# Attention probabilities turned by DMA transposes in place of TensorE transposes

## The chip, the cores and the metric

The kernel runs on one core of a Trainium2 chip. The metric is device time in microseconds (us) of one execution. The engines are TensorE (PE; its weight loads are listed apart as PEld), VectorE (DVE), ScalarE (ACT), GpSimd (POOL) and SyncE (SP). SP, ACT and POOL also issue DMA transfers, each in the order of its own queue; an entry that waits for something holds back all entries behind it on that queue.

## The reference

One decoder layer on 1024 tokens of width 1024. A normalised input is projected once; the columns feed two mixers, whose outputs are gated, projected, merged and added to the input. The part that matters here is mixer A: three groups of sliding-window attention with different window and dilation, eight heads each.

```python
qkv = dsa_qkv.astype(f32).reshape(b, s, DSA_GROUPS, 3, DSA_HEADS, DSA_HEAD_DIM)
q_a = _apply_rope(qkv[:, :, :, 0], cos, sin)
k_a = _apply_rope(qkv[:, :, :, 1], cos, sin)
v_a = qkv[:, :, :, 2]
# per group (window, dilation) = (128,1), (512,4), (2048,16):
scores = jnp.einsum('brnqhd,brnkhd->brnhqk', qb, kb) * (dh ** -0.5)
scores = jnp.where(valid[:, None], scores, -jnp.inf)
m = jnp.max(scores, axis=-1, keepdims=True)
p = jnp.exp(scores - m)
den = jnp.sum(p, axis=-1, keepdims=True)
o = jnp.einsum('brnhqk,brnkhd->brnqhd', p / den, vb)
# the three groups are merged by weights proportional to their denominators
```

Mixer B (gated DeltaNet), the gates and the output projection come after the attention stretch or share TensorE with it.

## The kernel before, in words

All projections run as split products: each float32 operand is written as a high and a low float16 part (`hi`, `lo`), and one product is three float16 matmuls (hi times hi, hi times lo, lo times hi; lines 182 to 184). The columns are cut in units of 256. For mixer A there is one q, one k and one v unit for each of six sets `(g, hs)`: group g in the order 2, 1, 0, and half hs of the heads (four heads each). A class `Feed` holds the units in order; one `tick` of it emits three matmuls of 512 columns or their equal. Weights of a unit come through two buffers `wstage` (one DMA each, issued by POOL, lines 161 and 312), and ACT and DVE split them into `whi` and `wlo`.

A finished q or k unit is rotated by DVE and ACT (`rope_half`) into tiles `pch`/`pcl`, and `rope_out` carries it in pieces of 32 partitions to the tiles `Qh`, `Ql` and `Ks`: 16 DMAs for a unit, and 2 more that copy a half for a q unit (lines 624 and 627).

Attention of one set is the generator `att_run`. It takes 16 steps: eight blocks j of 128 queries, and for each two passes `par`, with two heads in each (u = 0, 1). `nk` is the number of 128-key blocks that a query block sees: one in group 2, one or two in turn in group 1, two in group 0 except for the first block. A step s has three parts:

- `scores(s)`: four matmuls into a PSUM bank `ps_S` (two banks); then for each head a DVE instruction that masks, negates and takes the extreme in one go and writes the tile `sm` (line 794, called the reduce below), and an ACT exponential in place with its sum (line 798).
- `turn(s)`: PE transposes the probabilities, one 128x128 float32 block at a time, into a PSUM bank `ps_G` (line 808); ACT copies them to float16 (`th`, line 813), and DVE writes the remainder (`tl`).
- `values(s)`: matmuls of `th` and `tl` with the values `Vh`, `Vl` into the one bank `ps_O` (lines 831 to 835).

Iteration s of the loop emits `scores(s)`, `turn(s-1)` and `values(s-2)`, and yields a number of ticks (`pace`) behind each; `feed.run` puts that many ticks of projection matmuls there. PE's order is thus written out by hand. The order on DVE, ACT, POOL and SP is set by a scheduler that honours priorities; buffers (`bufs=2` and the like) add waits between engines. Results of groups 2 and 1 go to DRAM (`og`), and `combine` loads them back while group 0 runs (line 865, on SP).

Of the kernel before, what the change touches and what calls it, by code (L numbers as in the profile page):

```python
# [10 lines left out]
F32 = mybir.dt.float32  # L11
# [66 lines left out]
def hybrid_block(ctx: ExitStack, tc: tile.TileContext, A):  # L78
# [540 lines left out]
    def rope_out(pt, pieces):  # L619

        with tc.high_priority():
            for name, dst, r0, _ in pieces:
                for hd in range(4):
                    nc.sync.dma_start(out=dst[r0:r0 + 32, hd], in_=pt[name[1]][32 * hd:32 * hd + 32, "AB".index(name[0])])  # L624
# [128 lines left out]
    def att_run(g, hs, ts, pace):  # L753
# [17 lines left out]
        def scores(s):  # L771
# [10 lines left out]
            for u in range(2):  # L782
# [5 lines left out]
                          skip_group_check=True)  # L788
            P = ap.tile([128, 2, 256], F32, name="sm", tag="sm", bufs=2)
            Ps[s] = P  # L790
            for u in range(2):
                hd = 2 * u + par
                with tc.high_priority():
                    V.tensor_tensor_reduce(P[:, u, :128 * nk], psc[:, u * 256:u * 256 + 128 * nk], mask,  # L794
                                           -cexp, -NEG, ALU.add, ALU.min, accum_out=osb[:, 256 + hd:257 + hd])
            for u in range(2):
                hd = 2 * u + par
                SC.activation(P[:, u, :128 * nk], P[:, u, :128 * nk], AF.Exp, bias=osb[:, 256 + hd:257 + hd],  # L798
                              scale=-1.0, accum_out=osb[:, 260 + hd:261 + hd])

        def turn(s):
            nk = len(blocks(steps[s][0]))
            P = Ps.pop(s)
            pt = bank("G", 2)
            for u in range(2):
                for i in range(nk):
                    c = (u * nk + i) * 128
                    PE.transpose(pt[:, c:c + 128], P[:, u, i * 128:i * 128 + 128], ident)  # L808
            n = 256 * nk
            th = ap.tile([128, 512], F16, name="th", tag="th", bufs=2)  # L810
            tl = ap.tile([128, 512], F16, name="tl", tag="tl", bufs=2)
            with tc.high_priority():
                SC.copy(th[:, :n], pt[:, :n])  # L813
                TT(tl[:, :n], pt[:, :n], th[:, :n], ALU.subtract)
            ths[s] = th, tl

        def values(s):
            j, par = steps[s]
            kb = blocks(j)
            nk = len(kb)  # L820
            th, tl = ths.pop(s)
            if par == 0:
                pos[j] = bank("O", 1)
            po = pos[j]
            for u in range(2):
                hd = 2 * u + par
                out = po[:, hd * 64:hd * 64 + 64]
                vs = slice(hd * 64, hd * 64 + 64)
                for i, b in enumerate(kb):
                    c = slice((u * nk + i) * 128, (u * nk + i) * 128 + 128)  # L830
                    PE.matmul(out, lhsT=th[:, c], rhs=Vh[:, b, vs], start=(hd == 0 and i == 0), stop=False,
                              skip_group_check=True)
                    PE.matmul(out, lhsT=th[:, c], rhs=Vl[:, b, vs], start=False, stop=False,
                              skip_group_check=True)
                    PE.matmul(out, lhsT=tl[:, c], rhs=Vh[:, b, vs], start=False, stop=(i == nk - 1),
                              skip_group_check=True)
# [71 lines left out]
    gsp = {}  # L908
    gpool = [rp, "gst", 1]

# [21 lines left out]
    def gate_spill(br, dt, hf, p, rest=None):  # L932
        if (br, dt) not in gsp:
            gsp[br, dt] = tc.dram_tile([128, S], F32, name=f"gsp{br}{dt}")
        t = gpool[0].tile([128, 512], F32, name="gst", tag=gpool[1], bufs=gpool[2])
        if rest is not None:
# [114 lines left out]
    pre.append(pp_)  # L1051
    gpool[:] = pp_, "gst", 1
    def by_chunk(dst, x, hbs=(0, 1)):
# [585 lines left out]
    late.append(fp)  # L1639
    gpool[:] = fp, "gst", 2  # L1640
    gctx.close()
# [344 lines left out]
```

## Time and profile before

| | us |
|---|---|
| median of 3 runs | 1082.25 |
| the three runs | 1080.16, 1082.25, 1085.16 |
| span of the profiled execution | 1083.1 |
| PE busy in it | 1052.6 |
| DVE busy in it | 854.9 |
| ACT busy in it | 559.6 |
| POOL busy in it | 66.5 |

No time outside the span is listed for the profiled execution; its span stands 0.85 us above the median of the runs. Attention runs from about 100 us to 552 us of the span. In the views, a group row reads: line, engine, operation, tiles written and read, shape, count | busy us in all, mean ns of one | idle time of the engine ahead of them and what ended it. A window row reads: stretch, length, busy us (and count) of PE, PEld, DVE, ACT, POOL, then granted clock, DMA share and GB/s. Matmuls overlap in the pipeline, so the distance from one start to the next tells what one costs PE.

### The profile page before, as it was taken

The page shows a single profiled execution, that of the slowest core. Times are in us where ns is not written, and L with a number is a line of the kernel's source. Part 1 is how long each engine was busy: PE and PEld are TensorE (multiplying, and loading weights), DVE is VectorE, ACT ScalarE, POOL GpSimd, SP SyncE. Part 2 cuts the span into 40 slices and gives each one's busy share as a digit, 9 for nine tenths or more (in the row PEclk, how much of TensorE's full clock was granted, in tenths as well). Part 3 has the DMA queues.
Part 4 walks back from the last instruction along what each step waited for, and adds up shares of the span by engine and source line. Part 5 has one row for each costly group of instructions (what it writes and reads, how often), then busy time and mean ns, then how long its engine had stood idle before and what let it go on. Part 6 is the DMA issues. An engine that isn't in the chain of part 4 may idle for free.

```text
span 1083.1 us, 23724 instructions
## 1 busy us (share of the span) xinstructions
PE 1052.6 (97%) x9426; PEld 641.4 (59%) x9426; DVE 854.9 (79%) x1967; ACT 559.6 (52%) x1272; POOL 66.5 (6%) x115
## 2 busy tenths in 40 slices
PE   6999999999999999999999999999999999999997
PEld 6894595775966855765645544555545554444443
DVE  5697897878879778979965797976588778799934
ACT  6445766667666565557645534244454345333622
POOL 1200000000000000000000000110200000000000
PEclk9999999999999999999999999999999999999999
DMA  8135531632724431741233457785685523753232
GB/s 295 60 98 136 128 109 55 167 99 66 190 79 132 101 126 47 182 117 59 75 122 136 111 130 175 250 247 159 195 269 167 147 99 101 285 185 123 83 120 78
DMA packets 99632, 148.99 MB, mean 138 GB/s; under 512 B 31152, under 2 KB 64432, under 8 KB 98368
## 3 DMA queue, kind: packets, MB, share of 16 engines
q1 hardware_dynamic: 69264, 85.20, 27.3%
q0 software_dynamic: 12320, 44.11, 13.5%
q10 hardware_dynamic: 17936, 18.16, 4.9%
q8 instruction: 74, 1.21, 0.5%
q14 instruction: 38, 0.31, 0.1%
HBM read 91.66 MB, written 36.90 MB: 119 GB/s over the span
## 4 chain that ended last, share of the span: by engine, by line
PE 59%; DVE 26%; DMA 5%; ACT 4%; issue 3%; SPq 2%; ACTq 0%; DVEq 0%
PE ps_mm L182 14%; PE ps_mm L184 14%; PE ps_mm L183 14%; DVE ca L83 4%; DVE wlo L83 2%; DVE X L86 2%; DVE stmp L86 2%; DVE sm L794 2%; DVE rt L86 2%; PE ps_S L182 1%; PE ps_S L184 1%; PE ps_S L183 1%; DVE tl L86 1%; PE ps_G L808 1%; SPq L624 1%
## 5 line engine op out<-in xcount | busy, mean ns | idle before, releaser
L184 PE MATMUL ps_mm<-h_hi,wlo 128*128 128x512 f16 (+1 forms) x552 | 208.6, 378 | 1.2 <-issue 1.2
L183 PE MATMUL ps_mm<-h_lo,whi 128*128 128x512 f16 (+1 forms) x492 | 185.9, 378 | 1.0 <-DVE h_lo L86 1.0
L182 PE MATMUL ps_mm<-h_hi,whi 128*128 128x512 f16 (+1 forms) x492 | 186.0, 378 | 0.9 <-ACT h_hi L434 0.9
L184 PEld LDWEIGHTS <-wlo 128*128 128x128 f16 x788 | 77.5, 98 | 89.5 <-issue 3.4
L182 PEld LDWEIGHTS <-whi 128*128 128x128 f16 x848 | 83.4, 98 | 70.8 <-issue 0.5
L183 PEld LDWEIGHTS <-whi 128*128 128x128 f16 x848 | 83.4, 98 | 69.1 <-issue 2.2
L182 PE MATMUL ps_mm<-whi,h_hi 128*128 128x256 f16 x384 | 105.1, 274 | 0.0
L798 ACT ACTIVATE sm<-sm,osb 128x128 f32<-128x128 f32 (+1 forms) x160 | 69.5, 435 | 68.7 <-DVE osb L794 62.0
L184 PE MATMUL ps_mm<-whi,h_lo 128*128 128x256 f16 x384 | 104.7, 273 | 0.0
L183 PE MATMUL ps_mm<-wlo,h_hi 128*128 128x256 f16 x384 | 104.7, 273 | 0.0
L86 DVE TENSOR_TENSOR tl<-ps_G,th 128x256 f16<-128x256 f32 (+1 forms) x96 | 51.8, 540 | 21.5 <-ACT th L813 21.0
L794 DVE CUSTOM_DVE_ANT_0 sm<-ps_S,amask 128x128 f32<-128x128 f32 (+1 forms) x192 | 59.2, 345 | 8.5 <-PE ps_S L787 8.3
L83 DVE SCALAR_TENSOR_TENSOR wlo<-wstage,whi 128x1024 f16<-128x1024 f32 x50 | 60.8, 1218 | 4.4 <-ACT whi L165 4.1
L83 DVE SCALAR_TENSOR_TENSOR ca<-xc,cw,ca 128x512 f32<-128x512 f32 x72 | 53.7, 746 | 7.1 <-ACT ca L1001 6.3
L165 ACT ACTIVATE whi<-wstage 128x1024 f16<-128x1024 f32 x49 | 51.3, 1051 | 3.0 <-PE ps_O L183 1.4
L83 DVE SCALAR_TENSOR_TENSOR whi<-wstage,whi 128x512 f16<-128x512 f32 x60 | 40.8, 687 | 13.6 <-ACT whi L329 12.9
L808 PE MATMUL ps_G<-cons,sm 128*128 128x128 f32 x280 | 47.5, 275 | 2.1 <-ACT sm L798 1.0
L183 PEld LDWEIGHTS <-h_hi 128*128 128x128 f16 x384 | 45.8, 119 | 1.6
L329 ACT ACTIVATE whi<-wstage 128x512 f16<-128x512 f32 x60 | 37.1, 626 | 18.5 <-DVE wstage L328 13.4
L182 PE MATMUL ps_mm<-h_hi,wlo 128*128 128x512 f16 x120 | 45.6, 380 | 1.0 <-DVE rx L83 1.0
L182 PEld LDWEIGHTS <-h_hi 128*128 128x128 f16 x384 | 45.5, 119 | 1.5
L184 PEld LDWEIGHTS <-h_lo 128*128 128x128 f16 x384 | 45.5, 119 | 1.5
(436 smaller groups left out, 2584.4 us busy)
## 6 DMA issues: line engine op xcount, KB each, us to landing
wstage<-in_w POOLq DMA_DIRECT2D x68, 512.0 KB, 4.8
og<-osb ACTq DMA_DIRECT2D x32, 132.0 KB, 2.2
og<-og SPq DMA_DIRECT2D x32, 132.0 KB, 2.2
gspb<-gst ACTq DMA_DIRECT2D x16, 256.0 KB, 2.3
sga<-gspa SPq DMA_DIRECT2D x8, 512.0 KB, 6.9
wstage<-in_w_up POOLq DMA_DIRECT2D x8, 512.0 KB, 5.1
wos<-in_w_out SPq DMA_DIRECT2D x8, 512.0 KB, 5.4
sgb<-gspb SPq DMA_DIRECT2D x8, 512.0 KB, 5.9
```

Source lines behind the costliest of these rows:

```text
L83: (eng or V).scalar_tensor_tensor(out, in0, scalar, in1, op0=op0, op1=op1)
L86: (eng or V).tensor_tensor(out, in0, in1, op)
L165: in_turn(SC.activation(hi[:, 4 * c:4 * c + 4], st, AF.Copy, scale=W_SCALE))
L182: PE.matmul(out, lhsT=wh(k), rhs=mh(k), start=first and i == 0, stop=False, skip_group_check=True)
L183: PE.matmul(out, lhsT=wh(k), rhs=ml(k), start=False, stop=False, skip_group_check=True)
L184: last_pe[0] = PE.matmul(out, lhsT=wl(k), rhs=mh(k), start=False, stop=last and i == len(ks) - 1, skip_group_check=True).ins.name
L329: in_turn(SC.activation(t[:, b, 0], self.part[name], AF.Copy, scale=W_SCALE))
L624: nc.sync.dma_start(out=dst[r0:r0 + 32, hd], in_=pt[name[1]][32 * hd:32 * hd + 32, "AB".index(name[0])])
L794: V.tensor_tensor_reduce(P[:, u, :128 * nk], psc[:, u * 256:u * 256 + 128 * nk], mask, -cexp, -NEG, ALU.add, ALU.min, accum_out=osb[:, 256 ...
L798: SC.activation(P[:, u, :128 * nk], P[:, u, :128 * nk], AF.Exp, bias=osb[:, 256 + hd:257 + hd], scale=-1.0, accum_out=osb[:, 260 + hd:261 ...
L808: PE.transpose(pt[:, c:c + 128], P[:, u, i * 128:i * 128 + 128], ident)
```

## The change

The transposes on PE go. `sm` grows from 512 to 768 float32 columns: the probabilities stand in columns 256 and up; ACT writes their high float16 parts just below them, and DVE writes the low parts over their first half (each is behind what is read). One DMA transpose, issued by SP, turns both at once into a float16 tile `tT` (two buffers) with 4·nk blocks of 128x128. `values` reads `tT` and accumulates in one of the two banks `ps_G`; `turn_out` uses `ps_O`. The loop emits `values(s-3)` in place of `values(s-2)`, with slightly different yields. The piece DMAs of `rope_out` and the two loads of `combine` are issued by POOL in place of SP. The staging tile `gst` of a gate unit is taken from the pools `rx` and `ca` in place of one of its own.

```diff
@@ rope_out
-                    nc.sync.dma_start(out=dst[r0:r0 + 32, hd], in_=pt[name[1]][32 * hd:32 * hd + 32, "AB".index(name[0])])
+                    nc.gpsimd.dma_start(out=dst[r0:r0 + 32, hd], in_=pt[name[1]][32 * hd:32 * hd + 32, "AB".index(name[0])])
             for _, dst, r0, twice in pieces:
                 if twice and r0:
-                    nc.sync.dma_start(out=dst[64:128], in_=dst[0:64])
+                    nc.gpsimd.dma_start(out=dst[64:128], in_=dst[0:64])
@@ att_run, scores
-            P = ap.tile([128, 2, 256], F32, name="sm", tag="sm", bufs=2)
-            Ps[s] = P
+            n = 256 * nk
+            room = ap.tile([128, 768], F32, name="sm", tag="sm", bufs=2)
+            P = room[:, 256:256 + n].rearrange("p (u k) -> p u k", u=2)
+            Ps[s] = P, room.bitcast(F16)[:, 512 - n:512 + n]
...
@@ att_run, turn
-            P = Ps.pop(s)
-            pt = bank("G", 2)
-            for u in range(2):
-                for i in range(nk):
-                    c = (u * nk + i) * 128
-                    PE.transpose(pt[:, c:c + 128], P[:, u, i * 128:i * 128 + 128], ident)
-            n = 256 * nk
-            th = ap.tile([128, 512], F16, name="th", tag="th", bufs=2)
-            tl = ap.tile([128, 512], F16, name="tl", tag="tl", bufs=2)
+            P, both = Ps.pop(s)
+            hi, lo = [both.rearrange("p (l u k) -> p l u k", l=2, u=2)[:, l] for l in range(2)]
+            tT = ap.tile([128, 8, 128], F16, name="tT", tag="tT", bufs=2)
             with tc.high_priority():
-                SC.copy(th[:, :n], pt[:, :n])
-                TT(tl[:, :n], pt[:, :n], th[:, :n], ALU.subtract)
-            ths[s] = th, tl
+                SC.copy(hi, P)
+                TT(lo, P, hi, ALU.subtract)
+                nc.sync.dma_start_transpose(out=tT[:, :4 * nk], in_=both)
+            ths[s] = tT
@@ att_run, values
-                pos[j] = bank("O", 1)
+                pos[j] = bank("G", 2)
...
+                    th, tl = tT[:, u * nk + i], tT[:, 2 * nk + u * nk + i]
...
@@ att_run, loop
-        for s in range(n + 2):
+        for s in range(n + 3):
             if s < n:
                 scores(s)
                 yield pace[0]
             if 0 <= s - 1 < n:
                 turn(s - 1)
-                yield pace[1] + (s >= n)
-            if 0 <= s - 2 < n:
-                values(s - 2)
-                yield pace[2] + 2 * (s > n)
+            if s - 1 < n + 1:
+                yield pace[1]
+            if 0 <= s - 3 < n:
+                values(s - 3)
+                yield pace[2]
@@ combine
-            nc.sync.dma_start(out=og[:, i], in_=dram[g, hs][rows])
+            nc.gpsimd.dma_start(out=og[:, i], in_=dram[g, hs][rows])
...
-            pt = bank("G", 2)
+            pt = bank("O", 1)
@@ gates
-    gpool = [rp, "gst", 1]
+    gpool = [lambda: rope_room()[:, 0]]
...
-    gpool[:] = pp_, "gst", 1
+    gpool[0] = lambda: pp_.tile([128, 512], F32, name="gst", tag="ca", bufs=2)
```

How the instructions stand on three engines, before and after, at the places that the prediction speaks of.

On PE, in set (1, 1), ahead of a `values` call with nk = 1. `ps_mm` is a projection, L808 a transpose, L831 to L835 and L828 to L832 the value matmuls; square brackets hold what is waited for (DMAHW is a landed DMA of SP or ACT, DMASW one of POOL). Before:

```order
L184 LDWEIGHTS h_lo
L184 MATMUL ps_mm<-whi,h_lo 128x256
L808 MATMUL ps_G<-cons,sm 128x128 [waits PE_49,Activation_49]
L808 MATMUL ps_G<-cons,sm 128x128 [waits Activation_49]
L182 LDWEIGHTS h_hi
L182 MATMUL ps_mm<-whi,h_hi 128x256
...
L831 LDWEIGHTS th
L831 MATMUL ps_O<-Vh,th 128x64 [waits Activation_49]
L833 LDWEIGHTS th
L833 MATMUL ps_O<-Vl,th 128x64
L835 LDWEIGHTS tl [waits DVE_49]
```

After:

```order
L184 LDWEIGHTS h_lo
L184 MATMUL ps_mm<-whi,h_lo 128x256
L828 LDWEIGHTS tT [waits DMAHW0_49]
L828 MATMUL ps_G<-Vh,tT 128x64 [waits Activation_49]
L830 LDWEIGHTS tT
L830 MATMUL ps_G<-Vl,tT 128x64
L832 LDWEIGHTS tT
L832 MATMUL ps_G<-Vh,tT 128x64
```

The transposes between the projection matmuls are gone, and the first weight load of `values` waits for a DMA where it waited for ACT and DVE.

On DVE, in set (0, 1), two steps that follow each other; `osbs` takes the extremes, L83 `ca` is a convolution of mixer B that runs alongside. Before (buffer numbers are kept):

```order
L794 ISA sm_6961,osbs_6735<-ps_S_6956,amask_754 128x256 [waits PE_49]
L794 ISA osbs_6735 128x1
...
L86 TENSOR_TENSOR tl_6978<-ps_G_6972,th_6977 128x512 [waits Activation_49]
L86 TENSOR_TENSOR og_7008<-og_7008,f_7015 128x256
L83 SCALAR_TENSOR_TENSOR ca_6987<-xc_6984,cw_83,ca_6987 128x512 [waits Activation_49]
L794 ISA sm_7044,osbs_6735<-ps_S_7039,amask_754 128x256 [waits PE_49]
...
L86 TENSOR_TENSOR tl_7070<-ps_G_7064,th_7069 128x512 [waits Activation_49]
```

After:

```order
L796 ISA sm_6632,osbs_6430<-ps_S_6627,amask_754 128x256 [waits DMAHW6_49,PE_49]
L796 ISA osbs_6430 128x1
...
L83 SCALAR_TENSOR_TENSOR ca_6653<-xc_6650,cw_83,ca_6653 128x512 [waits Activation_49]
L86 TENSOR_TENSOR og_6601<-og_6601,f_6608 128x256
L83 SCALAR_TENSOR_TENSOR ca_6653<-xc_6650,cw_83,ca_6653 128x512 [waits DVE_49]
L86 TENSOR_TENSOR sm_6632<-sm_6632 128x512 [waits Activation_49]
L796 ISA sm_6687,osbs_6430<-ps_S_6682,amask_754 128x256 [waits DMAHW7_49,PE_49]
...
L86 TENSOR_TENSOR sm_6687<-sm_6687 128x512 [waits Activation_49]
```

Each reduce (L794, now L796) now waits for a DMA as well: the transpose that read the same `sm` buffer two steps ago. The low part of a step (`sm<-sm`) stands between the reduce of that step and the next one.

On POOL, between the k pieces of set (2, 1) and the q pieces of set (1, 0). Before, POOL held weight loads only:

```order
L161 DMA wstage<-in_w 128x1024 [waits DMASW6_49,DVE_49]
L312 DMA wstage<-in_w 128x1024 [waits DMASW7_49,DVE_49]
L312 DMA wstage<-in_w 128x1024 [waits DMASW0_49,DVE_49]
L312 DMA wstage<-in_w 128x1024 [waits DMASW2_49,DVE_49]
L312 DMA wstage<-in_w 128x1024 [waits DMASW1_49,DVE_49]
L161 DMA wstage<-in_w 128x1024 [waits DMASW4_49,DVE_49,Activation_49]
```

After:

```order
L624 DMA Ks<-pcl 32x1024 [waits DMASW6_49]
L863 DMA og<-og_733 128x264 [waits DMAHW4_49,DMAHW5_49,DMAHW3_49,DMAHW6_49,DMAHW2_49,DMAHW7_49,DMAHW1_49,DMASW7_49]
L312 DMA wstage<-in_w 128x1024 [waits DMASW0_49,DVE_49]
L312 DMA wstage<-in_w 128x1024 [waits DMASW1_49,DVE_49]
L161 DMA wstage<-in_w 128x1024 [waits DMASW1_49,DMASW2_49,DVE_49,Activation_49]
L161 DMA wstage<-in_w 128x1024 [waits DMASW3_49,DMASW0_49,DVE_49]
L624 DMA Qh<-pch 32x1024 [waits DMASW4_49,PE_49,Activation_49]
L624 DMA Qh<-pch 32x1024 [waits DMASW5_49]
```

Weight loads now share POOL's queue with the pieces and with a load that waits until the results of set (2, 0) have reached DRAM.

More of the change, by code (lines that the diff above doesn't have):

```diff
@@ L829, in values @@
                 for i, b in enumerate(kb):
-                    c = slice((u * nk + i) * 128, (u * nk + i) * 128 + 128)
-                    PE.matmul(out, lhsT=th[:, c], rhs=Vh[:, b, vs], start=(hd == 0 and i == 0), stop=False,
+                    th, tl = tT[:, u * nk + i], tT[:, 2 * nk + u * nk + i]
+                    PE.matmul(out, lhsT=th, rhs=Vh[:, b, vs], start=(hd == 0 and i == 0), stop=False,
                               skip_group_check=True)
-                    PE.matmul(out, lhsT=th[:, c], rhs=Vl[:, b, vs], start=False, stop=False,
+                    PE.matmul(out, lhsT=th, rhs=Vl[:, b, vs], start=False, stop=False,
                               skip_group_check=True)
-                    PE.matmul(out, lhsT=tl[:, c], rhs=Vh[:, b, vs], start=False, stop=(i == nk - 1),
+                    PE.matmul(out, lhsT=tl, rhs=Vh[:, b, vs], start=False, stop=(i == nk - 1),
                               skip_group_check=True)
@@ L1639, in hybrid_block @@
     late.append(fp)
-    gpool[:] = fp, "gst", 2
+    gpool[0] = lambda: fp.tile([128, 512], F32, name="gst", tag="gst", bufs=2)
     gctx.close()
```

8 lines of the change are left out of this document (4 added, 4 removed).

## The prediction

> **What bounds the kernel now.** I read the page's busy times first, then the chain that ended last, then busy time by stretch of the attention part, then who waited for whom in it.
>
> ```profile
> PE 1052.6 (97%) x9426; PEld 641.4 (59%) x9426; DVE 854.9 (79%) x1967; ACT 559.6 (52%) x1272; POOL 66.5 (6%) x115
> PE 59%; DVE 26%; DMA 5%; ACT 4%; issue 3%; SPq 2%; ACTq 0%; DVEq 0%
> ```
>
> PE is busy nearly throughout. The chain gives DVE a quarter, mostly outside the attention part. Of that part the stretches are (columns: PE, PEld, DVE, ACT, POOL busy, clock, DMA share, GB/s):
>
> ```profile
> 103.00:180.00 77.00, 76.06 (x606) 52.39 (x607) 61.08 (x164) 50.34 (x147) 2.11 (x4) 0.98 0.37 101
> 180.00:260.00 80.00, 80.00 (x650) 55.11 (x649) 66.69 (x157) 51.45 (x143) 3.17 (x6) 1.00 0.35 95
> ...
> 400.00:470.00 70.00, 67.90 (x570) 46.53 (x567) 64.08 (x178) 39.74 (x101) 3.69 (x7) 1.00 0.49 130
> 470.00:546.00 76.00, 73.81 (x683) 46.48 (x683) 67.87 (x241) 49.70 (x139) 2.11 (x4) 1.00 0.24 70
> sum 443.00, PE 437.78 PEld 299.87 DVE 374.20 ACT 280.85 POOL 17.94; mean PE 72.96 PEld 49.98 DVE 62.37 ACT 46.81 POOL 2.99
> ```
>
> PE idles 5 us of 443, so here a microsecond taken from PE is a microsecond of time, as long as nothing else is late. DVE stands at 84%, and at 92% and 89% in the last two stretches: there is little room behind PE. The waits of PE in this part are small:
>
> ```profile
> PE ps_O L835 <- DVE tl L86: 1.9, 2, 1.3
> PE ps_mm L182 <- DVE rx L83: 1.0, 1, 1.0
> ```
>
> How fast the steps follow each other is told by the first score matmuls (line 785), two to a step. In each set I took a stretch that holds whole steps; the count in brackets is twice the steps.
>
> ```profile
> 108.50:147.80 39.30, 3.97 (x24) 2.30 (x24) 1.00 0.49 130
> 174.60:217.80 43.20, 3.64 (x22) 2.10 (x22) 1.00 0.43 114
> 241.90:288.50 46.60, 4.44 (x22) 2.06 (x22) 1.00 0.43 117
> 313.90:360.50 46.60, 4.44 (x22) 2.08 (x22) 1.00 0.41 106
> 382.40:458.20 75.80, 6.38 (x26) 2.46 (x27) 1.00 0.40 110
> 493.30:540.70 47.40, 5.89 (x24) 2.38 (x25) 1.00 0.20 59
> ```
>
> So a step takes 3.27 us in set (2, 0), 3.93 in (2, 1), 4.24 in both sets of group 1, 5.83 in (0, 0) and 3.95 in (0, 1).
>
> **What is removed.** The 280 transposes:
>
> ```profile
> L808 PE MATMUL ps_G<-cons,sm 128*128 128x128 f32 x280 | 47.5, 275 | 2.1 <-ACT sm L798 1.0 <-DVE tl L86 0.7
> 308.42 0.38 PE L808 MATMUL ps_G<-cons,sm 128*128 128x128 f32 x2
> 308.64 0.38 PE L182 MATMUL ps_mm<-sum2h,wlo 128*128 128x512 f16 x1
> ```
>
> The group's 47.5 us counts overlap. From the start of two transposes to the start of the next matmul are 0.22 us, so one costs 0.11 us and all cost 30.8 us. By set that is 16 steps of 0.22 us in group 2 (3.5 us a set), 48 blocks or 5.3 us in each set of group 1, and 60 blocks or 6.6 us in each of group 0.
>
> **What is added: a ring through the DMA.** The rest of a step is the same work in another place:
>
> ```profile
> L794 DVE CUSTOM_DVE_ANT_0 sm<-ps_S,amask 128x256 f32<-128x256 f32 x88 | 33.5, 417 | 1.3 <-PE ps_S L787 1.3
> L794 DVE CUSTOM_DVE_ANT_0 sm<-ps_S,amask 128x128 f32<-128x128 f32 x104 | 25.7, 284 | 7.2 <-PE ps_S L787 7.1
> L798 ACT ACTIVATE sm<-sm,osb 128x128 f32<-128x128 f32 x100 | 39.5, 395 | 35.8 <-DVE osb L794 34.4 <-issue 1.3
> L798 ACT ACTIVATE sm<-sm,osb 128x256 f32<-128x256 f32 x60 | 30.0, 501 | 32.9 <-DVE osb L794 27.6 <-issue 5.4
> L798 ACT ACTIVATION_READ_ACCUMULATOR sm<-sm,osb 128x1 f32 x160 | 30.0, 188 | 0.0
> L813 ACT CAST th<-ps_G 128x512 f16<-128x512 f32 x44 | 24.9, 565 | 1.0 <-PE ps_G L808 0.8
> L813 ACT CAST th<-ps_G 128x256 f16<-128x256 f32 x52 | 18.5, 357 | 2.7 <-PE ps_G L808 1.8 <-ACT osb L840 0.8
> L86 DVE TENSOR_TENSOR tl<-ps_G,th 128x512 f16<-128x512 f32 x44 | 30.1, 683 | 5.4 <-ACT th L813 5.1
> L86 DVE TENSOR_TENSOR tl<-ps_G,th 128x256 f16<-128x256 f32 x52 | 21.8, 419 | 16.1 <-ACT th L813 15.9
> ```
>
> From a free `sm` buffer to the finished low part a step needs one reduce, two exponentials with their sums, the high part and the low part: 0.28 + 2 x 0.58 + 0.36 + 0.42 = 2.2 us with nk = 1, and 0.42 + 2 x 0.69 + 0.57 + 0.68 = 3.0 us with nk = 2. I add 0.7 us for handing over and queueing (an estimate: ACT sat idle about 62 us before 160 exponentials for DVE, 0.4 us each, and the rest for the other hops): C = 2.9 and 3.7 us. That the split reads SBUF and not PSUM I cost at nothing.
>
> Then the transpose runs for a time L from its issue to its landing, and only then may the reduce two steps on write the same buffer, since `sm` has two. So two steps take at least L + C. The transpose also waits for `values` two steps back (`tT` has two buffers), which does not add to the ring: PE is by then past it. Behind the waiting reduce stand, on DVE, the evictions of projections, the weight splits and the rotations; PE waits for the first.
>
> No row shows a transposing DMA. The nearest rows, for issue to landing:
>
> ```profile
> og<-osb ACTq DMA_DIRECT2D x32, 132.0 KB, 2.2
> Ks<-pch SPq DMA_DIRECT2D x40, 64.0 KB, 2.1
> m_d<-MT SPq DMA_DIRECT2D x8, 128.0 KB, 3.9
> MT<-u_d SPq DMA_DIRECT2D x8, 128.0 KB, 7.5
> ```
>
> With nk = 2 the source is 128 partitions of 2 KB, which in pieces of 128 numbers is 1024 short runs; `m_d` and `MT` move 1024 short runs each (32x32 rows of 32 numbers) and rearrange across partitions. So L is between 2.2 us (a plain transfer) and 7.5 us. I take 3.9, the store with as many runs, since it reads SBUF as the transpose does. For nk = 1, half the runs, I take 3.0, the middle of 2.1 and 3.9. The Trainium skill, "DMA: Bandwidth & Descriptors", section Latency and other measured facts, gives a transposing DMA 261 GB/s; with the 2 us fixed cost of the same page that is an estimate of 3.0 us for the larger one, by which the set (0, 1) below would gain its full 6.6 us and the sum be some 4 us better. No trace here shows it yet.
>
> The least step by the ring is (3.0 + 2.9) / 2 = 2.95 us in group 2, (3.0 + 3.9 + 2.9 + 3.7) / 4 = 3.4 in group 1 and (3.9 + 3.7) / 2 = 3.8 in group 0. PE without transposes would need 3.05, 3.71, 3.91, 3.91, 5.42 and 3.54. The larger of both rules: only set (0, 1) is held by the ring, and gains 16 x 0.15 = 2.4 us in place of 6.6. Gains: 3.5 + 3.5 + 5.3 + 5.3 + 6.6 + 2.4 = 26.6 us.
>
> **What is given back.** Set (0, 0) would shrink by 7% where DVE is at 92%, so at 98%; I give back half of its excess, 2.5 us. For the reduces that now stand waiting ahead of evictions I take one PE wait of 0.4 us for each of some 20 units in this part, 8 us (today one such wait of 1.0 us; the ends are 0 and 20). The extra iteration of each set is covered by ticks, except at the last one, where some 2 us may show.
>
> **What moves to POOL.** SP loses some 200 piece DMAs and 32 loads; POOL gains them.
>
> ```profile
> L624 SPq DMA_DIRECT2D Qh<-pch x48: 507/589/2087, 68.8 to 441.5; - x48
> L161 POOL DMA_DIRECT2D wstage<-in_w x38 | 20.1, 530 | 389.8 <-DVE wlo L83 194.0 <-DVE wstage L328 80.3 <-DVE xc L998 72.2
> POOL wstage L312 <- DVE whi L83: 134.5, 4, 40.4
> ```
>
> Issue costs 0.53 us on POOL against 0.59 on SP, so a unit's 18 pieces take 9.5 us; at least a v unit lies between the k pieces and their use. Weight loads waited up to 40 us on POOL for their buffer, so they are early by tens of microseconds; the pieces and `og` loads in front of them fit in that cover. I cost it at nothing, and if the cover is gone it is the third rival. The banks, the staging tile and the removed `ps_G` waits are within 1 us.
>
> **The sum.** 26.6 - 2.5 - 8 - 2 = 14 us off the profiled 1083.1, so 1069; the median of the runs is 0.85 us below that execution, so 1068 to 1069.
>
> **Rivals.**
>
> *Slower, by a long transpose.* If L is as that of `MT<-u_d`, 7.5 us, and 4.8 us with nk = 1 (half way from 2.1), the ring sets the step: 3.85 us in group 2, 4.73 in group 1, 5.6 in group 0. Against today: +9, -1, +8, +8, -4 and +26 us, with the give-backs of 10 us some +56, so 1139. It decides from about L = 5.2 us with nk = 2 on: there (0, 1) loses 8 us, (2, 0) nothing, and the gain of the rest just pays the give-backs. For it speaks that other queues use 35 to 49% of the DMA time here; against it that the plain transfers of this size land in 2 us beside the same traffic. The Trainium skill speaks against the change too: "VectorE: DVE Perf Modes", The three transpose paths, gives 1309 ns for one 128x128 block by DMA and 390 ns on TensorE, and says to use TensorE where a PSUM destination is fine; the trace's 275 ns, 0.11 from start to start, agrees with the cheap side. Were eight blocks to go one after the other at that price, L would be 10.5 us, an estimate, and the kernel above 1200 us.
>
> *No change.* DVE sets the pace: in the new order the low part of a step stands ahead of the next reduce, so a step is no shorter than C plus what DVE does between, about 3.3 us and 4.0 us with nk = 1 and 2 if only 0.3 us of other work comes between. Group 2's first set and set (0, 1) then gain nothing, the others half: 10 us gained, 10 given back, 1080 to 1085.
>
> *Slower, by POOL.* If weight loads come 2 us late for 20 units because POOL stands at a piece or an `og` load, 40 us are lost: 1109. Against it: those 40 us of slack.
>
> **How the numbers follow.** Forecast (faster) 0.47; no change 0.20; long transpose 0.26; POOL 0.07. A measurement of this kernel tells about 0.5%, 5.4 us. The forecast's own range is 1053 (all 30.8 us gained) to 1076. The whole range goes up to 1122, which leaves out the worse half of the long transposes. Faster 0.47, same 0.20, slower 0.33.
>
> **What would show it.** The transposes' issue to landing is the first thing: under 5 us with nk = 2 for the forecast. Step times in the six sets near 3.05, 3.7, 3.9, 3.9, 5.5 and 3.8 us. PE's waits on `tT` and on DVE in the attention part under 15 us in all; the reduces' waits for DMA may be long without harm. POOL's weight loads should still be waiting for buffers, not PE for weights. The prediction is wrong if PE waits for `tT` or `ps_S` at most steps (long transposes), or if PE is slack with DVE at 95% or more.

## The result: 6.1% slower, lost at the ends of the sets

The changed kernel takes 1150.23 us (median of 4 runs, 1145.88 to 1153.01) against 1083.7 us for the kernel before (1080.16 to 1087.56) beside it: a ratio of 1.0609, 95% interval [1.0574, 1.0643]. It is 66 us slower, where 14 us of gain were forecast. The profiled execution has a span of 1144.1 us, 61.0 more than before.

Busy times, and the chain that ended last, on the page of the changed kernel:

```profile
PE 1044.3 (91%) x9146; PEld 615.4 (54%) x9146; DVE 857.6 (75%) x1967; ACT 567.3 (50%) x1272; POOL 184.9 (16%) x351
PE 61%; DVE 16%; DMA 15%; ACT 4%; issue 3%; SPq 0%; DVEq 0%; POOL 0%; ACTq 0%
```

The 280 transposes are gone from PE (9426 matmuls before, 9146 now), but PE is busy only 8 us less. The chain's DMA share went from 5% to 15%. DVE and ACT are as busy as before, and POOL's 118 us more go with the DMAs that it now issues: the new time is waiting. The whole attention part in one row, of the kernel before and then of the changed one (the columns are those of the stretches in the prediction):

```profile
100.00:552.00 452.00, 443.05 (x3742) 302.76 (x3741) 379.78 (x1032) 287.11 (x773) 18.46 (x35) 1.00 0.39 107
```

```profile
98.00:612.00 514.00, 433.44 (x3448) 275.18 (x3446) 382.48 (x1027) 293.79 (x771) 118.91 (x235) 0.94 0.62 130
```

All of the loss is here: 514 us against 452. PE idles 80.6 us against 9.0. Its busy time fell by 9.6 us where the transposes alone were worth 30.8, so the rest of its work took some 21 us longer, and the granted clock says why: 0.94 against 1.00. The stretches at a clock of 0.50, taken together, are 59.65 us after, with PE busy in 40.09 of them, and one of 3.42 us before:

```profile
sum 59.65, PE 40.09 PEld 23.66 DVE 41.05 ACT 26.62 POOL 14.15; mean PE 3.64 PEld 2.15 DVE 3.73 ACT 2.42 POOL 1.29
104.07:107.49 3.42, 3.42 (x13) 1.49 (x12) 1.50 (x5) 1.44 (x8) 0.00 (x0) 0.50 0.00 0
```

At half the clock the work takes twice its time (the same 128x256 matmuls start every 0.11 us at 501 us and every 0.21 us at 516 us), so half of the 36.7 us between them, some 18 of the 21 us, is the clock's (an estimate). The account is +71.6 idle, +21 longer work, -30.8 transposes: +62 us.

Where in the part? From the start of each step's first score matmul in the two traces (us):

| set | (2,0) | (2,1) | (1,0) | (1,1) | (0,0) | (0,1) |
|---|---|---|---|---|---|---|
| a step, steps 3 to 8, before | 3.31 | 3.85 | 4.18 | 4.18 | 5.64 | 3.95 |
| the same, after | 2.99 | 3.66 | 3.83 | 3.83 | 5.64 | 4.13 |
| a step, steps 9 to 15, before | 3.27 | 3.99 | 4.26 | 4.25 | 6.04 | 3.92 |
| the same, after | 4.02 | 4.53 | 4.45 | 4.88 | 6.85 | 5.09 |
| last scores to the next set's first, before | 15.2 | 11.6 | 12.6 | 12.6 | 26.7 | |
| the same, after | 22.1 | 18.6 | 17.7 | 18.7 | 39.8 | |

The middle of the first four sets runs as forecast. The late steps do not, and the gaps between sets grew by 6.9, 7.0, 5.1, 6.1 and 13.1 us, 38 us of the 60 between the first scores and the last. What PE waited for between 98 and 612 us (engine, line, releaser: us in total, times, longest):

```profile
PE ps_G L828 <- DMA tT<-sm: 48.5, 25, 4.1
PE ps_O L892 <- DVE mx L86: 12.7, 1, 12.7
PE ps_O L892 <- DVE osbs L86: 6.0, 1, 6.0
PE ps_S L787 <- issue: 4.7, 1, 4.7
DVE sm L796 <- DMA tT<-sm: 47.7, 23, 5.8
```

The first matmul of `values` stands before a transpose that has not landed; twice PE stands before the transposes of the combination, whose vectors are late on DVE. The last line is DVE's: its reduces wait for transposes too. The longest of these waits ends at 494.7 us, after a transpose of 13.5 us; DVE then works without a break from 503 to 514 us, and nearly all of PE's 12.7 us lie in that stretch. How long a transpose takes, for all of them (min, median, max), and then in two stretches of set (1, 0), the quiet one and the end, with what else moved:

```profile
L811 SPq DMA_TRANSPOSE tT<-sm x96: 1189/1232/3781, 106.1 to 608.3; - x96
DMA to landing us min/median/max: 2.4/3.8/13.5
```

```profile
wstage<-in_w POOLq DMA_DIRECT2D x2, 512.0 KB, 5.1
Qh<-pch POOLq DMA_DIRECT2D x4, 64.0 KB, 3.2
tT<-sm SPq DMA_TRANSPOSE x9, 2.7
```

```profile
wstage<-in_w POOLq DMA_DIRECT2D x2, 512.0 KB, 6.9
tabs<-in_tabs SPq DMA_DIRECT2D x1, 1024.0 KB, 5.0
Qh<-Qh POOLq DMA_DIRECT2D x1, 512.0 KB, 6.2
Ql<-Ql POOLq DMA_DIRECT2D x1, 512.0 KB, 5.5
Qh<-pch POOLq DMA_DIRECT2D x4, 64.0 KB, 7.3
tT<-sm SPq DMA_TRANSPOSE x4, 7.1
```

From 258 to 295 us nine transposes land after 2.7 us in the middle; from 295 to 315 us, beside two weight loads and the queries' pieces, four take 7.1 us, and the loads too are slower than in the quiet stretch. (The load of a table, `tabs`, is issued at 314.1 us, when three of the four have landed; at the end of set (1, 1), 371 to 388 us, no table is loaded and the middle is 7.1 us as well.) In sets (2, 1) to (0, 0) this comes at the same place, from step 9 on, because the feed makes the next set's q unit there; in set (2, 0) it begins at step 5. The last set has no next q unit, and its transposes from step 9 on land after 3.0 to 4.3 us.

There is a second place. Of PE's 48.5 us, 21.5 stand before the `values` of the last two steps of a set, with no scores left between a turn and its values. From the issue of these transposes until PE comes to them are at most 4.3 us, but for one of 6.9, and twice PE is there first; in the middle of sets (2, 1) to (1, 1) some 7 us lie between. At the end of set (2, 0), 165.5 to 171 us, the two land as fast as in any quiet part, beside one store, and PE still waits for both:

```profile
og<-osb ACTq DMA_DIRECT2D x1, 132.0 KB, 1.8
tT<-sm SPq DMA_TRANSPOSE x2, 2.4
...
PE ps_G L828 <- DMA tT<-sm: 3.9, 2, 2.8
```

So two things come together at a set's end: the burst of loads, pieces and copies makes transposes long, and the drain (the iterations behind the last scores) is too short even for a quick one.

The clock's part is seen around one such wait, at the end of set (1, 1) (stretch, length, busy times, then clock, DMA share, GB/s):

```profile
388.00:392.00 4.00, 0.15 (x4) 0.15 (x5) 0.12 (x2) 0.00 (x0) 0.00 (x0) 0.99 0.84 134
392.00:394.00 2.00, 2.00 (x20) 1.57 (x19) 2.00 (x7) 1.70 (x7) 0.00 (x0) 0.50 0.03 8
394.00:396.00 2.00, 2.00 (x14) 1.56 (x13) 1.93 (x7) 1.84 (x5) 0.69 (x2) 0.67 0.32 65
396.00:398.00 2.00, 2.00 (x25) 1.81 (x24) 1.67 (x3) 1.69 (x5) 2.00 (x5) 1.00 0.59 128
...
406.00:408.00 2.00, 1.21 (x14) 0.92 (x15) 0.66 (x1) 0.35 (x2) 0.00 (x0) 0.50 0.15 52
408.00:410.00 2.00, 2.00 (x7) 0.64 (x5) 1.42 (x3) 1.58 (x4) 0.00 (x0) 0.50 0.26 78
410.00:412.00 2.00, 2.00 (x6) 0.72 (x5) 0.48 (x1) 0.00 (x0) 1.10 (x2) 0.50 0.20 47
```

PE waits from 388 to 392 us, and runs the next 3.4 us at half its clock. After a wait of 2.1 us that ends at 404.1 us it runs at half clock from 405.6 to 412.4 us. A wait here costs more than itself. The Trainium skill, "TensorE: Matmul & The Clock Gate", Part 1: The HAM clock gate, says that the clock is halved after an idle window of about 3.4 us and comes back after a busy one, and that the window runs freely. The trace agrees on the window: all changes of the clock lie on one grid of 3.41 us, and half clock lasts 3.4 or 6.8 us, once 13.7. It differs on the idle time, and here the trace decides: that time need not fill the window. In this part every halving follows a window in which PE idled 1.96 us or more, and none follows one with 1.77 us or less. So a wait of 2.3 us (at 129.7) halved the clock, since it lay within one window, and a longer one of 3.0 us (at 233.5) did not, since the edge at 234.9 us parts it. The windows around the two:

```profile
129.09:132.50 3.41, 1.11 (x11) 0.48 (x10) 0.42 (x3) 0.79 (x3) 0.17 (x1) 1.00 0.93 187
132.50:135.92 3.42, 3.42 (x13) 1.49 (x11) 3.42 (x10) 1.72 (x6) 0.08 (x1) 0.50 0.20 41
231.49:234.90 3.41, 2.02 (x19) 1.76 (x17) 1.70 (x2) 0.00 (x0) 0.00 (x0) 1.00 1.03 192
234.90:238.32 3.42, 1.85 (x24) 1.85 (x25) 1.73 (x6) 1.40 (x6) 0.00 (x0) 1.00 0.38 41
238.32:241.73 3.41, 3.41 (x38) 3.40 (x36) 3.31 (x9) 2.21 (x7) 0.49 (x1) 1.00 0.19 38
```

### The profile page after: what moved, and what is told of

It is laid out like the page before. It is cut to its first block, busy times and chain, and to the rows that moved or that the text cites. A ratio compares the mean times of both kernels' runs of the same rounds, so it can differ in the third digit from the quotient of the medians.

```text
span 1144.1 us, 23445 instructions
## 1 busy us (share of the span) xinstructions
PE 1044.3 (91%) x9146; PEld 615.4 (54%) x9146; DVE 857.6 (75%) x1967; ACT 567.3 (50%) x1272; POOL 184.9 (16%) x351
## 2 busy tenths in 40 slices
DMA packets 168239, 167.33 MB, mean 146 GB/s; under 512 B 105904, under 2 KB 135088, under 8 KB 166976
## 4 chain that ended last, share of the span: by engine, by line
PE 61%; DVE 16%; DMA 15%; ACT 4%; issue 3%; SPq 0%; DVEq 0%; POOL 0%; ACTq 0%
PE ps_mm L182 15%; PE ps_mm L183 14%; PE ps_mm L184 14%; DMA tT<-sm 13%; DVE sm L796 2%; DVE rt L86 2%; ACT sm L800 2%; DVE sm L86 2%; PE ps_S L184 1%; PE ps_S L183 1%; PE ps_S L182 1%; DVE wlo L83 1%; DMA oa_d<-osb 1%; PE ps_S L477 1%; PE ps_G L183 1%
## 5 line engine op out<-in xcount | busy, mean ns | idle before, releaser
L182 PE MATMUL ps_mm<-h_hi,whi 128*128 128x512 f16 (+1 forms) x492 | 189.9, 386 | 0.9 <-ACT h_hi L434 0.9
L183 PE MATMUL ps_mm<-h_lo,whi 128*128 128x512 f16 (+1 forms) x492 | 189.3, 385 | 1.0 <-DVE h_lo L86 1.0
L796 DVE CUSTOM_DVE_ANT_0 sm<-ps_S,amask 128x128 f32<-128x128 f32 (+1 forms) x192 | 59.8, 349 | 68.0 <-DMA tT<-sm 47.7
L182 PE MATMUL ps_mm<-whi,h_hi 128*128 128x256 f16 x384 | 108.1, 282 | 0.0
L183 PE MATMUL ps_mm<-wlo,h_hi 128*128 128x256 f16 x384 | 107.7, 281 | 0.0
L828 PE MATMUL ps_G<-Vh,tT 128*128 128x64 f16 x280 | 36.7, 199 | 49.2 <-DMA tT<-sm 48.5
L86 DVE TENSOR_TENSOR sm<-sm 128x256 f16<-128x256 f32 (+1 forms) x96 | 52.2, 544 | 21.4 <-ACT sm L809 21.2
L83 DVE SCALAR_TENSOR_TENSOR wlo<-wstage,whi 128x1024 f16<-128x1024 f32 x50 | 60.8, 1221 | 8.6 <-ACT whi L165 8.5
L161 POOL DMA_DIRECT2D wstage<-in_w x38 | 20.5, 540 | 259.3 <-DVE wlo L83 100.6
L828 PEld LDWEIGHTS <-tT 128*128 128x128 f16 x280 | 27.0, 101 | 62.6 <-DMA tT<-sm 57.2
L83 DVE SCALAR_TENSOR_TENSOR ca<-xc,cw,ca 128x512 f32<-128x512 f32 x72 | 53.9, 749 | 7.7 <-ACT ca L999 6.8
L83 DVE SCALAR_TENSOR_TENSOR whi<-wstage,whi 128x512 f16<-128x512 f32 x60 | 40.7, 690 | 18.8 <-ACT whi L329 18.5
L809 ACT CAST sm<-sm 128x256 f16<-128x256 f32 (+1 forms) x96 | 48.0, 500 | 1.6
L183 PEld LDWEIGHTS <-h_hi 128*128 128x128 f16 x384 | 46.7, 122 | 2.3
```

Source lines behind the costliest of these rows:

```text
L83: (eng or V).scalar_tensor_tensor(out, in0, scalar, in1, op0=op0, op1=op1)
L86: (eng or V).tensor_tensor(out, in0, in1, op)
L161: (eng or nc.gpsimd).dma_start(out=st, in_=src[:, 4 * c:4 * c + 4])
L182: PE.matmul(out, lhsT=wh(k), rhs=mh(k), start=first and i == 0, stop=False, skip_group_check=True)
L183: PE.matmul(out, lhsT=wh(k), rhs=ml(k), start=False, stop=False, skip_group_check=True)
L796: V.tensor_tensor_reduce(P[:, u], psc[:, u * 256:u * 256 + 128 * nk], mask, -cexp, -NEG, ALU.add, ALU.min, accum_out=osb[:, 256 + hd:257 + ...
```

## The experiments

Each was run in turn with the kernel before; a ratio is to that kernel. The letters stand for: A, the transposes are long at the sets' ends and badly covered there; B, GpSimd's queue makes pieces and weights late; A1 to A4, finer forms of A (A1 too few ticks at a set's end, A2 traffic whatever the ticks, A3 two `tT` buffers, A4 two `sm` buffers); T, the transposes wait behind the weight loads.

**Pieces back on SyncE** (in the changed kernel):

```
-  nc.gpsimd.dma_start(out=dst[r0:r0 + 32, hd], ...)     (and the copies, and og)
+  nc.sync.dma_start(out=dst[r0:r0 + 32, hd], ...)
```

> The changed kernel with the pieces and the loads for the combination back on SyncE's queue, beside the transposes. Theory A (the transposes get long wherever weight loads and pieces fill the DMA, which is at the end of each set, and there fewer ticks lie between a turn and its values): the transposes still run beside the same bytes, and the pieces now stand behind transposes that wait for DVE, so 1135 to 1175 us; TensorE's waits for tT at 90 us or more. Theory B (GpSimd's queue in order makes pieces, loads and weights late): most of the loss goes, 1085 to 1115 us.

1147.91 us, ratio 1.0576 [1.0538, 1.0615]: as A says. PE's waits at line 828 are still 43.0 us (96.5 with those of its weight loads, which is how the expectation counts them). GpSimd's queue is not where the 66 us are.

**Only the pieces moved** (the same lines, the other way, in the kernel before):

> The kernel before, with nothing changed but that GpSimd issues the pieces and the loads for the combination. Theory A: 1080 to 1092 us, TensorE idle under 15 us from 100 to 552 us. Theory B: 1105 us or more, with TensorE waiting for weights, scores or the combination.

1090.83 us, ratio 1.0045 [1.0022, 1.0069]. A, with a price of some 5 us. The trace, of the shortest of the ten runs, shows half of it: the first scores of set (2, 0) wait 4.9 us for the last copy of the queries (`Ql`, landed at 103.5 us) where they waited 2.3 us before (PE's waits from 95 to 615 us):

```profile
PE ps_S L787 <- issue: 4.9, 1, 4.9
```

**Late steps by TensorE** (in the changed kernel; the banks of before):

```
+  if s < 9:
       ... SC.copy(hi, P); TT(lo, ...); nc.sync.dma_start_transpose(out=tT[:, :4 * nk], in_=both)
+  else:
+      ... PE.transpose of each block into pt = bank("G", 2)
+      SC.copy(tT[:, :2 * nk], pv); TT(tT[:, 2 * nk:4 * nk], pv, tT[:, :2 * nk], ALU.subtract)
```

> The changed kernel, in which steps 9 to 15 of each set are turned by TensorE again (fp32 transposes into PSUM, then the halves written into the same tT), steps 0 to 8 by DMA; the banks are those of before. Theory A: the waits at the ends of the sets (49 us of the 81 us that TensorE idles in the attention part) go, about 10 us of clock come back, and 7/16 of 30.8 us of transposes are paid again: 1095 to 1115 us. Theory B: 1140 to 1165 us. If the transposes of the early steps are the trouble: 1125 us or more.

1111.62 us, ratio 1.0247 [1.0224, 1.0269], in A's range. Seven of sixteen steps, with the banks, bring 38.6 us although 128 transposes (14 us) are paid again: on the DMA the late steps cost some 53 us (an estimate). The gaps between the first five sets fall to 15.1, 12.8, 13.7 and 13.9 us.

**The order without the transposes** (all steps by TensorE, `s < 0` above, pieces on SyncE):

> All steps turned by TensorE and pieces on SyncE as before, but values one step later, with the ticks of the changed kernel and its tT tiles: the order of the change without its transposes. Theory A: 1078 to 1095 us. If the order itself (one more iteration at each set's end) is the cost: 1105 us or more.

1092.25 us, ratio 1.0067 [1.0043, 1.0090]. The order with `values` one step later costs 7 us, most of it in the last gap (33.6 us against 26.7), where PE waits 7.1 us before the combination's transposes. The other gaps are within 0.4 us of those before.

**More ticks at a set's end**:

```
-  yield pace[1]          and, behind values,   yield pace[2]
+  yield pace[1] + 2 * (s >= n)                 yield pace[2] + 2 * (s >= n)
-  (left + 0.5) / (16 * sum(pace) + 3)
+  (left + 0.5) / (16 * sum(pace) + 13)
```

> The changed kernel with two more ticks of other work at each stop of the iterations after a set's last scores (10 a set; the rate before them is lowered by as much). Theory A1 (at a set's end too few ticks lie between a turn and its values): the gap from a set's last scores to the next set's first ones shrinks by 3 us or more at each of the four like transitions, TensorE's waits for tT fall from 106 to under 70 us (TensorE and its weight loads counted together), and with the clock that comes back 1115 to 1135 us. Theory A2 (the transposes are long there because of the traffic, and what is moved behind one only moves the wait): 1140 to 1155 us.

1148.85 us, ratio 1.0591 [1.0564, 1.0618]. PE's waits for `tT` fell as A1 said (PE 28.7 us, its loads 35.5 us), and the time did not: the reduces wait 58.8 us for transposes, and PE waits 7.3 us for pieces of the keys. The wait moved, as A2 had it.

**Three `tT` buffers** and **three `sm` buffers**. Both needed room, taken from `og` (one buffer in place of two) and, for `sm`, also from `osb` (three in place of four); the third run has only what was taken for `sm`.

> The changed kernel with three tT buffers (og has one in place of two to make room, which touches group 0 alone). Theory A3 (the transpose starts late because it waits for the values two steps back): SyncE's 40 us of waits for ps_G go, the gaps between the sets of groups 2 and 1 shrink by 2 us or more each, 1120 to 1140 us. Theory A1: gaps within 1 us of 22.1, 18.6, 17.7, 18.7, and 1143 to 1160 us (up to 8 us of it for og).

> The changed kernel with three sm buffers (og has one in place of two, osb three in place of four, to make room). Theory A4 (the ring by sm: the reduce that waits for a transpose holds DVE, and with it evictions and the combination): the reduces' 48 us of waits for DMA fall under 10 us, TensorE's waits for the combination (12.7 and 6.0 us) go, 1115 to 1138 us. Theory A1: the reduces' waits fall too, but TensorE's waits for tT stay at 80 us or more, 1140 to 1160 us.

> The changed kernel with og in one buffer and osb in three, the room that the run with three sm buffers took, and nothing else. If sm was right and the loss there came from og: 1175 to 1195 us, the first four sets as in the changed kernel (58.8, 80.0, 77.2, 79.2 us). If the third buffer itself cost time: 1148 to 1160 us.

1181.59 us (ratio 1.0886 [1.0859, 1.0913]), 1167.38 (1.0770 [1.0737, 1.0804]) and 1186.32 (1.0938 [1.0899, 1.0978]). Taken by themselves the first two miss every expectation: the room came from a place that costs 36 us, most of it from set (0, 0) on, which I had put at 8 at most. Against the third run, three `sm` buffers are worth 19 us. In the sets that `og` does not touch, (2, 0) to (1, 1), from one set's last scores to the next's (the first from its own first scores), three `sm` buffers give 57.6, 69.4, 73.2 and 73.6 us; the changed kernel 58.8, 80.0, 77.2 and 79.2; the control 57.4, 80.9, 80.4 and 81.8; the kernel before 50.9, 70.6, 71.0 and 72.0; three `tT` buffers 58.5, 78.1, 78.4 and 81.7. So A4 and not A3. It was to be shown without the loss in `og`:

**Three rooms of `sm` and nothing taken but one of the two small buffers `sml`**. The high halves of a step lie in front of its probabilities; the rooms overlap there, in a part that is dead by then:

```
-  room = ap.tile([128, 768], F32, name="sm", tag="sm", bufs=2)
+  room = ring[:, s % slots * 512:s % slots * 512 + 768]     # ring: 512 * slots + 256; 3 slots, 2 in the last set
```

> The changed kernel with room for three steps of sm in the first five sets (buffers that overlap in the part that is dead by then, so nothing else is made smaller but sml, to one buffer); the last set keeps two. Theory A4 (a set's last transposes take 5 to 9 us beside the weight loads, two buffers then hold the reduce, and behind it on DVE stand the evictions that PE waits for): the first four sets last as with three buffers before (57.6, 69.3, 73.3 and 73.5 us from start to start), set (0, 0) loses less than 104 us, 1115 to 1132 us. Theory A1 (the values at a set's end come too soon after their transpose, buffers or not): 1138 to 1150 us.

(The set times named there run from last scores to last scores, as above.) 1129.73 us, ratio 1.0414 [1.0374, 1.0453]: A4, 20 us of the 66. Those times are 53.1, 70.1, 71.6 and 77.0 us now. The reduces' wait for transposes fell from 47.7 us to

```profile
DVE sm L801 <- DMA tT<-sm: 21.4, 21, 3.1
```

but PE still waits for `tT`, and longer before the combination:

```profile
PE ps_G L833 <- DMA tT<-sm: 35.5, 21, 4.0
PE ps_O L897 <- DVE mx L86: 16.6, 1, 16.6
PE ps_O L897 <- DVE osbs L86: 9.0, 2, 7.6
```

`sml` is a tile of the combination; whether its one buffer has a part in the longer wait there was not tried.

**The combination's transposes 30 ticks later**, not 20 (`TURN_LAG`), on top of it:

> Three rooms of sm (1129.7 us before) and the transposes of the combination 30 ticks behind its start in place of 20. TensorE stood 16.6 and 7.6 us before two of these. Theory (at the end of group 0's sets the combination's chain on DVE is late behind reduces that wait, and TensorE comes to its transposes by count of ticks, too soon): those two waits fall under 6 us in all, 1102 to 1116 us with the clock. If DVE is late by any count: 1124 us or more.

1127.26 us, ratio 1.0407 [1.0360, 1.0454]: the time is in the second range (1124 us or more), and no shorter than 1129.73 beyond the noise. The waits before the combination did fall, from 25.6 to 6.1 us. They moved: PE's waits for `tT` are 38.1 us in place of 35.5, it stands 6.0 us before scores that wait for reduces, and steps 9 to 15 of set (0, 0) take 6.6 us in place of 5.4. That DVE is late by any count is one reading of this, and not shown.

**Early steps by DMA in the order of before**, with two and with three rooms of `sm`:

```
+  dma = [g > 0 and s < 8 for s in range(16)]
   for s in range(n + 2): ...
+      for k in range(n):
+          if s == k + 2 + dma[k]: values(k)
```

> The order of before (values two steps behind the scores, ticks at the end as before, pieces on SyncE), but steps 0 to 7 of the four sets of groups 2 and 1 turned by DMA with values three steps behind; all other steps by TensorE. Takes 80 of the 280 transposes off TensorE, 8.8 us. Theory A (only transposes at the sets' ends and in group 0 are badly covered): 1073 to 1081 us, faster than before. If transposes that run in the quiet part lose too (clock, waiting reduces): 1083 to 1095 us.

> Steps 0 to 7 of the first four sets turned by DMA, the rest by TensorE in the order of before, pieces on SyncE (the earlier run of this gave 1101 us), now with three rooms of sm in the first five sets. Theory A4: the handover from DMA to TensorE at steps 8 to 11 no longer stalls (5 to 9 us a step there), 1076 to 1087 us, near or under the kernel before. Else 1095 us or more.

1101.1 us (1.0156 [1.0130, 1.0182]) and 1088.94 (1.0061 [1.0034, 1.0089]). The first is a miss for me: even 80 transposes fewer in the quiet part lose. The second falls between its two ranges. With two rooms the steps at the handover take up to 8.8 us, since the next PE transposes wait for reduces that wait for the DMA; the third room takes 12 us of that back. Neither beats the kernel before. No version here that does all the work does.

**Half of each transpose**:

```
-  nc.sync.dma_start_transpose(out=tT[:, :4 * nk], in_=both)
+  nc.sync.dma_start_transpose(out=tT[:, 2 * nk:4 * nk], in_=both[:, 256 * nk:])
```

> The changed kernel, but only the low half is turned, and the values use it in place of the high half too (this leaves out the high part; PE's work is the same): half the bytes of every transpose. If the time that a transpose takes and the load it puts on the DMA go with its size: issue to landing falls to 2.4 us or less in the quiet parts and to 3 to 5 us at the sets' ends, 1095 to 1125 us. If the latency is that of waiting in line with other traffic, whatever the size: 1138 to 1150 us.

1137.67 us, ratio 1.0494 [1.0461, 1.0527], just under the range for waiting in line. Landing in two stretches of set (1, 0), 255 to 291 us and 291 to 308 us:

```profile
tT<-sm SPq DMA_TRANSPOSE x9, 2.4
...
tT<-sm SPq DMA_TRANSPOSE x3, 6.8
```

Half the bytes take 2.4 us in place of 2.7 where it is quiet and 6.8 in place of 7.1 at the end. The time is mostly latency and waiting, and little of it size; all the same the kernel is 12.6 us faster than the changed one.

**No weight loads in the attention part**, in the changed kernel and in the one before:

```
+  if kept: return kept[c]        # the two staging tiles of the first unit, again and again
```

> The changed kernel without the weight loads of the attention part: every unit there splits the same two staging tiles again (this leaves out the weights' loads, all other work stays). Theory T (the transposes wait in line behind the 512 KB loads, whatever their own size): issue to landing at the sets' ends falls from 5 to 9 us to 2.4 to 4 us, the reduces' waits for DMA go, 1090 to 1115 us. If it is the pieces, or the transposes among themselves: 1130 to 1150 us.

> The kernel before without the same weight loads, as the measure for the run above. TensorE is busy there anyway: 1075 to 1088 us. By theory T the difference of the two runs is under 30 us, against 66 us with loads.

1116.67 us (1.0297 [1.0260, 1.0334]) and 1080.79 (0.9970 [0.9950, 0.9990]). The loads cost the kernel before some 3 us and the changed one 33.6: without them the change loses 36 us in place of 66, so nearly half of its loss hangs on them. T holds only in part: it had the difference under 30 us, landing within 4 us, and no more waits of the reduces, which are still 22.7 us. Landing at the end of set (1, 0), 280 to 302 us, is 5.3 us in the middle, beside pieces and copies, two stores, and from 297.6 us a table:

```profile
tabs<-in_tabs SPq DMA_DIRECT2D x1, 1024.0 KB, 5.1
Qh<-Qh POOLq DMA_DIRECT2D x1, 512.0 KB, 4.5
Ql<-Ql POOLq DMA_DIRECT2D x1, 512.0 KB, 6.9
og<-osb ACTq DMA_DIRECT2D x2, 132.0 KB, 2.9
Ql<-pcl POOLq DMA_DIRECT2D x4, 64.0 KB, 2.6
Qh<-pch POOLq DMA_DIRECT2D x3, 64.0 KB, 3.1
tT<-sm SPq DMA_TRANSPOSE x4, 5.3
```

The longest of the four, 8.9 us, is issued at 286.3 us, while the two copies of 512 KB are under way and no load is. So weight loads are not needed to make a transpose long.

**No loads, three rooms, pieces on SyncE, all at once**:

> The three causes found so far taken away together: the attention part's weight loads left out (the weights are those of the first unit), three rooms of sm in the first five sets, pieces and combination loads on SyncE; the transposes stay on the DMA. Measure: the kernel before without the loads, 1080.8 us. Of the change's 66 us, 5 were GpSimd's, 20 the third buffer's, 30 the loads'. If these add up, 1091 to 1100 us, and what is left is the order with one more iteration. If they are the same microseconds counted twice: 1105 to 1117 us, and the end of the sets stays too short for a transpose even without traffic.

1120.56 us, ratio 1.0332 [1.0300, 1.0363]: no better than without the loads alone, and 3.6 us above the upper range. The parts do not add up. That a late step is in time with a short transpose or with a third room, and gains nothing from both, would explain it; it is argued, not shown. What stays is in the gaps between sets (19.5, 13.7, 18.5, 18.0 and 37.7 us, 28.7 us in all over those before), in these waits of PE:

```profile
PE ps_G L838 <- DMA tT<-sm: 34.3, 21, 4.0
PE ps_O L902 <- DVE mx L86: 11.0, 1, 11.0
PE ps_O L902 <- DVE sml L86: 7.5, 1, 7.5
```

A part of this is the short drain again: some 13 of the 34.3 us stand before the last two steps of the sets, and at the end of set (1, 1) PE waits 2.4 us for a transpose that lands after 3.0 us. So the end of a set is too short for 3 us as well. How much of the rest is the pieces' own traffic (single transposes near the end of four sets still take 5 to 7 us) stays open: a kernel without the pieces was not tried.

## Why the prediction was wrong

*What a transpose on PE costs, and what the middle of a set gains: right in the first four sets.* Steps of 3.05, 3.7, 3.9, 3.9 and 5.5 us were forecast for the first five sets; steps 3 to 8 take 2.99, 3.66, 3.83, 3.83 and 5.64. Set (0, 0) gained nothing there, with one step of 7.7 us, and the last set lost: 4.13 after 3.95 before, where 3.8 was forecast.

*The time L of a transpose: the step that failed, not in its value but in taking one value for a set.* I took 3.0 and 3.9 us; in quiet parts it is 2.4 and 3.0 to 3.1, better than I took. (The estimate worked out from the Trainium skill's "DMA: Bandwidth & Descriptors", 3.0 us for the larger, fits there; the 1309 ns a block from "VectorE: DVE Perf Modes" do not apply one after the other, since eight blocks land in 3.0 us.) Late in each of the first five sets it is 5 to 9 us, in set (0, 0) up to 13.5. Against the rival I had set that "the plain transfers of this size land in 2 us beside the same traffic": a median over the whole run, which hides that the loads and the pieces of the next q unit come in one burst. With L = 7.1 my own ring gives (7.1 + 3.3) / 2 = 5.2 us a step of group 1, whose mean C is 3.3, where PE needs 3.9; I had put the L from which it decides at 5.2. The rival by a long transpose (1139) was the right mechanism in the late steps only, and it had no term for the drain; that its time lies near the measured one is in part luck. The third room shows what the ring by `sm` costs (20 us), the run without loads what the loads of this part cost (33.6 us); both together give no more than the second.

*"The extra iteration of each set is covered by ticks, except at the last one": the second step that failed.* I put down 2 us for it; the gaps between sets grew by 38 us in all, long transposes included. Without DMA transposes the same iteration costs 7 us, most of it in the last gap: the ticks cover a turn on PE, and neither a landing of 5 us or more nor, in the last two steps, a quick one of 2.4 us. More ticks there cut those two steps' waits from 21.5 to 8.3 us and did not help, since then the reduces wait.

*The give-backs.* For waiting reduces I gave back 8 us, with an end of 20; they alone wait 47.7 us for transposes, and what that costs shows in PE's waits at lines 828 and 892. DVE as the bound in set (0, 0), for which I gave back 2.5 us, came up in another form: over the part it is busy 382 of the 514 us, but after its longest wait for a transpose it works without a break from 503 to 514 us while PE stands.

*The move to POOL at nothing: mis-sized.* By itself in the kernel before it costs some 5 us; 2.6 of them are seen at the first scores of set (2, 0), where PE waits 4.9 us in place of 2.3. "At least a v unit lies between the k pieces and their use" left out the copies of that set's queries, for which PE waited already before.

*The clock is in no term.* The sum had PE's work at full clock throughout. Once PE waits 2 to 4 us at a time, the clock adds some 18 us.

*What would show it.* PE's waits on `tT` and DVE were to stay under 15 us in all; they are 48.5 and 18.7.

*Two slips without effect.* All 30.8 us gained would be 1052 us of the profiled execution, not 1053; and C plus 0.3 us is 3.2 us with nk = 1, not 3.3.

## What to carry to other kernels

Work that is moved from a busy engine to a DMA gets that DMA's latency at the worst moment, not in the median: look for the stretch in which the other transfers come in a burst, and ask whether the ring and the drain hold there. A pipeline's end has less cover than its middle (here at most 4.3 us against some 7), so price it by itself. And an idle stretch of a few microseconds on TensorE cost its clock afterwards as well, here some 18 us on top of 71.6.

## What the runs showed of the hardware

A transposing DMA from SBUF to SBUF kept SyncE 1.2 us for each issue (up to 3.8), and landed after 2.4 us with 128 KB and 3.0 to 3.1 with 256 KB where little else moved; half the size saved 0.1 and 0.6 us there and 0.3 in a burst. The packets under 512 B rose from 31152 to 105904, 779 for each transpose in the mean:

```profile
DMA packets 168239, 167.33 MB, mean 146 GB/s; under 512 B 105904, under 2 KB 135088, under 8 KB 166976
```

TensorE's granted clock changed on a grid of 3.41 us only, went to 0.50 after a window with 1.96 us or more of idle time, and stayed there for 3.4 or 6.8 us, once 13.7. And one buffer less for the loads of the combination, with one less of `osb`, cost 36 us, more than half of the change itself.
